# First attention: two units taken together, both scored, a pair multiplied by the values, another pair turned

## The chip, the cores and the metric

The kernel runs on one core of a Trainium2 chip. The metric is the device time of one execution in microseconds (us). Five engines matter: PE (TensorE: matmuls and transposes), PEld (its weight loads, shown as a row of their own), DVE (VectorE), ACT (ScalarE), POOL (GpSimd), and the DMA queues, of which SP's carries most loads.

## The reference

A model of three blocks with 1024 channels, on 1024 latent tokens and 256 context tokens. The change lies in the first block's attention, which has two parts, both computed for every tile of 128 query tokens:

- part A: 8 heads of 64 with 2 key heads (four heads share one). A latent query sees the keys of its own block of 128, of the blocks on either side where they are within 128 tokens, and all 256 context keys; a context query sees the context keys alone. A sink value joins the sum of each softmax.
- part B: 4 heads with two score sets each, `w = softmax(s1) - lam * softmax(s2)`, and `w @ v` with values of 128. A latent query sees all 1280 keys, a context query the 256 context keys.

Cut to what matters:

```python
def sink_attention(qg, k, v, sink, valid):
    s = einsum('bqhgd,bkhd->bhgqk', qg, k) * 64 ** -0.5
    s = where(valid, s, NEG_INF)
    p = softmax(concatenate([s, sink_col], -1), -1)[..., :-1]
    return einsum('bhgqk,bkhd->bqhgd', p, v)

def diff_attention(q1, q2, k1, k2, v, lam):
    s1 = einsum('bqhd,bkhd->bhqk', q1, k1) * 64 ** -0.5
    s2 = einsum('bqhd,bkhd->bhqk', q2, k2) * 64 ** -0.5
    w = softmax(s1, -1) - lam * softmax(s2, -1)
    return einsum('bhqk,bkhe->bqhe', w, v)
```

The outputs of both parts are normed and gated, and go through an output matrix in the next stage.

## The kernel before

`layer0` first projects queries, keys, values and gates and stores them in device memory, then does the attention. There are ten query tiles, in the order `ORD` = 0, 1, 2, 3, 8, 9, 4, 5, 6, 7; 8 and 9 are the context tiles. Each tile has two halves of six units: four A heads (`a_scores`) and two B heads (`b_scores`), in the order A0, B0, A1, A2, B1, A3 (the very first half begins with B0, A0). That makes 120 units. A unit has three steps:

- scores, at once when `a_scores` or `b_scores` is called. PE multiplies queries by keys (L685, L687 for A, L730, L731 for B) in single-pass fp32r; for a latent A unit one or two bf16 matmuls add the window masks (L690, L692). DVE reads the scores out of PSUM with their minimum (L695; L732, L734), ACT takes the exponentials (L697; L736, twice for B), and for B DVE combines both score sets (L740, L741, L742). The weights stand then in a tile `Pa` or `Pb0`.
- `turns`: PE transposes the weights, block by block of 128 keys (L663, in `turn`; five blocks for a latent A unit of an inner tile, four in tiles 0 and 7, two for context queries; ten for B, two for context queries). ACT copies the result out of PSUM into `PTa` or `PTb` (L665), for B's second group DVE does (L667).
- `outs`: PE multiplies the transposed weights by the values. A does it in two halves of 64 columns that stand side by side in the array (L710, a 128x64 form); B with whole columns of 128 (L754).

```python
                for j, b in enumerate(kbl):
                    for u in range(2):
                        nc.tensor.matmul(t.o[64 * u:64 * u + 64, hh * 64:(hh + 1) * 64], PT[:, j, 64 * u:64 * u + 64],
                                         V[:, b, g * 64:(g + 1) * 64], start=(j == 0), stop=(j == len(kbl) - 1))
```

An fp32 matmul by values runs as two instructions, so a latent A unit has 20 of L710 (16 in tiles 0 and 7, 8 for context queries) and a latent B unit 20 of L754.

PSUM has eight banks: two buffers `sc` of two banks for the large scores (an A unit takes one, a B unit one for each of its score sets e0 and e1), one buffer `scc` for the 256 context scores of B, and three buffers `tp` for transposed blocks, one of which holds the half's output `t.o` from the first `outs` to `half_end`. In SBUF there are four `Pa`, two of each `Pb`, three `PTa` and two `PTb`. `half_end` scales, norms and gates a half's output on DVE, ACT and POOL. `head_of_tile` loads the next tile's queries `Q` (L582, four transfers on SP's queue) and gates.

The loop at the end of `layer0` is a hand-written pipeline over units. In step n it scores unit n, turns unit n - 3 (`LAGA` = 3) and multiplies unit n - 4 by the values; `half_end` follows each sixth unit, and the head of the next tile is loaded in step 8 of the 12 of a tile. After the last scores the query buffers are given back, and `Bridge` begins with the output stage: it loads its weights, and one step later transposes the first attention output (L876).

The order on each engine is that in which the compiler's scheduler places the instructions: mostly the written order, but where an instruction isn't ready by its account (a buffer that isn't free yet), later ones go ahead.

Of the kernel before, what the change touches and what calls it, by code (L numbers as in the profile page):

```python
# [23 lines left out]
EPS = 1e-6  # L24
NEG = -1e30
LAM0 = 0.2
LAGA = 3
ORD = (0, 1, 2, 3, 8, 9, 4, 5, 6, 7)
WB = 8

# [262 lines left out]
def rstd_of(k, pool, ss, n, inv_n, name):  # L293

    nc = k.nc
    r = pool.tile([128, n], F32, name=name)
    nc.vector.tensor_scalar(r, ss, inv_n, EPS, op0=OP.mult, op1=OP.add)
    nc.gpsimd.tensor_tensor(r, r, k.mhalf[:, :n], op=OP.pow)
    return r
# [146 lines left out]
def layer0(k, x, ctxt):  # L446
# [13 lines left out]
    with ExitStack() as es:  # L460
# [116 lines left out]
        def load_q(i):  # L577

            Q = qp.tile([128, 16, 2, 128], F32R, name="Q", bufs=2)
            for part in range(2):  # L580
                for u in (0, 64):
                    nc.sync.dma_start(Q.bitcast(F32)[u:u + 64, :, part, :], dq[i][64 * part:64 * part + 64])  # L582
            return Q
# [51 lines left out]
    with ExitStack() as es:  # L635
# [12 lines left out]
        def head_of_tile(i):  # L648

            t = Ctx()  # L650
            tiles[i] = t
            t.Q = Q0 if i == order[0] else load_q(i)
            t.gt = p.tile([128, 1024], F32, name="gt", bufs=2)
            nc.sync.dma_start(t.gt, dg[i])
            t.mt = p.tile([128, 1024], F32, name="mt", bufs=2)
            t.sta = p.tile([128, 8, 4], F32, name="sta", bufs=2)
            t.stb = p.tile([128, 4, 8], F32, name="stb", bufs=2)
            t.o = None
# [99 lines left out]
        def half_end(i, hg):  # L758

            t = tiles[i]  # L760
            ca, cb = slice(256 * hg, 256 * hg + 256), slice(512 + 256 * hg, 768 + 256 * hg)
            h4, h2 = slice(4 * hg, 4 * hg + 4), slice(2 * hg, 2 * hg + 2)
            es_ = p.tile([128, 4], F32, name="esk", bufs=2)
            nc.vector.tensor_add(es_, sink[:, h4], t.sta[:, h4, 0])
            nc.scalar.activation(es_, es_, AF.Exp)
            nc.vector.tensor_add(es_, es_, t.sta[:, h4, 2])
            rl = p.tile([128, 6], F32, name="rl", bufs=2)
            nc.vector.reciprocal(rl[:, 0:4], es_)
            nc.vector.reciprocal(rl[:, 4:6], t.stb[:, h2, 2])
            ma, mb = t.mt[:, ca], t.mt[:, cb].rearrange("p (h d) -> p h d", d=128)  # L770
            nc.vector.tensor_mul(ma.rearrange("p (h d) -> p h d", d=64), t.o[:, 0:256].rearrange("p (h d) -> p h d", d=64),  # L771
                                 rl[:, 0:4, None].to_broadcast([128, 4, 64]))
            nc.vector.tensor_mul(mb, t.o[:, 256:512].rearrange("p (h d) -> p h d", d=128), rl[:, 4:6, None].to_broadcast([128, 2, 128]))
            t.o = None
            nc.gpsimd.tensor_mul(ma, ma, t.gt[:, ca])  # L775
            sq = p.tile([128, 2, 128], F32, name="sqb", bufs=1)
            ss = p.tile([128, 2], F32, name="ssb", bufs=2)
            nc.gpsimd.tensor_mul(sq, mb, mb)
            nc.vector.tensor_reduce(ss, sq, axis=AX.X, op=OP.add)
            rr = rstd_of(k, p, ss, 2, 1.0 / 128, "rrb")  # L780
            nc.gpsimd.tensor_mul(mb, mb, subg[:, None, :].to_broadcast([128, 2, 128]))
            nc.gpsimd.tensor_mul(t.mt[:, cb], t.mt[:, cb], t.gt[:, cb])
            nc.vector.tensor_mul(mb, mb, rr[:, :, None].to_broadcast([128, 2, 128]))
            if hg:
                nc.sync.dma_start(dm[i], t.mt)

        units = []
        order = list(ORD)
        for i in order:
            for hg in range(2):  # L790
                a, b = 4 * hg, 2 * hg
                u = [(a_scores, i, a), (b_scores, i, b), (a_scores, i, a + 1), (a_scores, i, a + 2), (b_scores, i, b + 1),
                     (a_scores, i, a + 3)]
                if not units:
                    u[0], u[1] = u[1], u[0]
                units += u
        head_of_tile(order[0])
        fs = []
        for n in range(len(units) + LAGA + 1):
            if n < len(units):  # L800
                f, i, h = units[n]
                fs.append(f(i, h))
                if n % 12 == 8 and i != order[-1]:
                    head_of_tile(order[n // 12 + 1])
            if n == len(units):

                es0.close()
                k.slots = Slots(k)
                br = Bridge(k, 0, (0, 1), dm, NTC)
                br.fetch(p.tile([128, S + L], F32, name="Pb1", bufs=2)[:, :D])  # L810
                br.start(k.slots)
            if 0 <= n - LAGA < len(units):
                fs[n - LAGA][0]()
            j = n - LAGA - 1
            if j >= 0:
                fs[j][1]()
                if j % 6 == 5:
                    half_end(units[j][1], j // 6 % 2)
            if n == len(units) + 1:
                br.first(lambda: ps.tile([128, 4, 128], F32, name="tp", bufs=3),  # L820
                         lambda b: p.tile([128, 2, 4, 128], F32R, name=("gt", "mt")[b], bufs=2))
    br.es = es2
# [1452 lines left out]
def body(tc, nc, A, out):  # L2275
    k = Ctx()
    k.tc, k.nc, k.A, k.ndma = tc, nc, A, 0
    squeeze(A)
    tiles = lambda ap, n: [ap[i * 128:(i + 1) * 128, :] for i in range(n)]
    with ExitStack() as es:  # L2280
        setup(k, es)
        x1, x2 = ([k.dr.tile([128, D], F32, name=f"{n}_{i}") for i in range(NT)] for n in ("x1", "x2"))
        x, ctxt = tiles(A["x"], NT), tiles(A["ctx"], 2)
        br = layer0(k, x, ctxt)
        br = layer1(k, br, x, ctxt, x1)
        dm = mixer2(k, br, x1, x2)
        moe(k, dm, x2, tiles(out, NT))
# [27 lines left out]
```

## Time and profile before

| | |
|---|---|
| median of 3 runs | 2800.44 us (2799.43 to 2801.71) |
| profiled execution, its own time | 2795.24 us |
| its span | 2793.5 us |
| mean granted TensorE clock | 0.979 of 2.4 GHz |
| PE busy | 2645.3 us (95% of the span) |
| DVE, ACT, POOL busy | 1536.0, 1066.6, 580.9 us |

The attention runs from about 487 to 858 us of the span. In the rows of PE a matmul's duration contains its way through the array, and the next one starts before it ends; what a group of matmuls takes is read from its start to the start of the next group.

### The profile page before, as it was taken

Reading aid. Unit: us, or ns where it says so; the run is one execution under the profiler, and the core shown is the slowest. Engines: PE = TensorE matmul, PEld = TensorE weight load, DVE = VectorE, ACT = ScalarE, POOL = GpSimd, SP = SyncE. Lnnn points to the kernel's source line nnn. Section 1 sums busy time; section 2 is a strip of 40 time slices with the busy share of each in tenths; the row PEclk is TensorE's granted clock in tenths of the full one; section 3 lists DMA queues with packets and bytes.
Section 4 is the critical chain, followed back from the end, with each engine's and each line's share of the span. In section 5 each row is a group of like instructions: output and inputs, shape, how many; then the busy total and the mean of one; then the engine's idle time right before and its main releaser. Section 6 shows DMA issues by size and latency. Waiting matters only on the chain. (4 is left out here: it accounts for less than half of the span.)

```text
span 2793.5 us, 41767 instructions
## 1 busy us (share of the span) xinstructions
PE 2645.3 (95%) x15970; PEld 2172.5 (78%) x15970; DVE 1536.0 (55%) x2972; ACT 1066.6 (38%) x2035; POOL 580.9 (21%) x515
## 2 busy tenths in 40 slices
PE   8999999999999999999999999999999999969995
PEld 3777778887887778887887887788878977857774
DVE  5467747887886461100884434373206655357886
ACT  4333321666663332112642332222316621246563
POOL 1334400012211110012541120000000033025662
PEclk9999999999999999999999999999999999979998
DMA  7233387546224353222654123232437157449995
GB/s 249 83 90 106 114 214 213 183 92 121 66 51 164 108 184 106 86 76 101 200 193 151 60 84 106 91 117 83 125 122 174 32 165 253 143 171 325 312 317 173
DMA packets 273570, 405.33 MB, mean 145 GB/s; under 512 B 28338, under 2 KB 156585, under 8 KB 272721
## 3 DMA queue, kind: packets, MB, share of 16 engines
q1 hardware_dynamic: 255360, 365.79, 42.7%
q0 software_dynamic: 6624, 24.14, 3.4%
q10 hardware_dynamic: 11376, 12.64, 1.4%
q8 instruction: 128, 2.10, 0.3%
q14 instruction: 82, 0.66, 0.1%
HBM read 290.35 MB, written 112.15 MB: 144 GB/s over the span
## 5 line engine op out<-in xcount | busy, mean ns | idle before, releaser
L164 DVE TENSOR_TENSOR slotl<-slotraw,sloth 128x1024 fp32r<-128x1024 f32 (+2 forms) x100 | 116.8, 1170 | 282.7 <-ACT sloth L161 226.6
L168 PE MATMUL pj<-sloth,u2h 128*128 128x512 f32 (+1 forms) x592 | 237.4, 401 | 0.0
L169 PE MATMUL pj<-slotl,u2h 128*128 128x512 f32 (+1 forms) x592 | 234.8, 397 | 0.0
L170 PE MATMUL pj<-sloth,u2l 128*128 128x512 f32 (+1 forms) x592 | 233.2, 394 | 0.0
L168 PE MATMUL pj<-wh,h0h 128*128 128x512 f32 (+1 forms) x560 | 216.2, 386 | 0.3 <-DVE h0h L338 0.3
L169 PE MATMUL pj<-wl,h0h 128*128 128x512 f32 (+1 forms) x560 | 212.3, 379 | 0.5 <-DVE wl L164 0.4
L170 PE MATMUL pj<-wh,h0l 128*128 128x512 f32 (+1 forms) x560 | 211.4, 378 | 0.0
L169 PE MATMUL pj<-slotl,h1h 128*128 128x512 f32 x432 | 168.7, 391 | 0.0
L168 PE MATMUL pj<-sloth,h1h 128*128 128x512 f32 x432 | 168.7, 390 | 0.0
L170 PE MATMUL pj<-sloth,h1l 128*128 128x512 f32 x432 | 168.5, 390 | 0.0
L161 ACT CAST sloth<-slotraw 128x1024 fp32r<-128x1024 f32 (+2 forms) x100 | 99.6, 999 | 152.8 <-PE my L170 62.5
L168 PEld LDWEIGHTS pj<-sloth,u2h 128*128 128x128 f32 (+1 forms) x592 | 110.0, 186 | 28.3 <-issue 1.0
L170 PEld LDWEIGHTS pj<-sloth,u2l 128*128 128x128 f32 (+1 forms) x592 | 110.0, 186 | 28.3
L169 PEld LDWEIGHTS pj<-slotl,u2h 128*128 128x128 f32 (+1 forms) x592 | 110.0, 186 | 26.8 <-issue 1.0
L168 PEld LDWEIGHTS pj<-wh,h0h 128*128 128x128 f32 x560 | 106.7, 191 | 20.7 <-issue 2.0
L169 PEld LDWEIGHTS pj<-wl,h0h 128*128 128x128 f32 x560 | 107.1, 191 | 19.4 <-DVE wl L164 1.6
L170 PEld LDWEIGHTS pj<-wh,h0l 128*128 128x128 f32 x560 | 106.4, 190 | 19.6
L164 DVE TENSOR_TENSOR w13l<-raw,w13h 128x1024 fp32r<-128x1024 f32 x51 | 106.0, 2092 | 1.6 <-ACT w13h L161 1.1
L736 ACT ACTIVATE Pb<-Pb,stb 128x1280 f32<-128x1280 f32 (+1 forms) x80 | 94.9, 1188 | 29.9 <-DVE stb L735 29.6
L168 PE MATMUL pj<-sloth,omTh 128*128 128x512 f32 x256 | 103.3, 404 | 0.5 <-ACT omTh L161 0.5
L775 POOL TENSOR_TENSOR mt<-mt,gt 128x256 f32<-128x256 f32 x20 | 14.7, 737 | 422.9 <-DVE mt L771 219.6
L170 PE MATMUL pj<-sloth,omTl 128*128 128x512 f32 x256 | 101.6, 398 | 0.0
(614 smaller groups left out, 6707.9 us busy)
## 6 DMA issues: line engine op xcount, KB each, us to landing
raw<-in_exp_w_dram SPq DMA_DIRECT2D x102, 512.0 KB
Q<-dq SPq DMA_DIRECT2D x40, 512.0 KB
slotraw<-in_w_in_dram SPq DMA_DIRECT2D x40, 512.0 KB
mraw<-in_adaln_w_dram SPq DMA_DIRECT2D x64, 256.0 KB
wraw<-in_ab_w_in_dram SPq DMA_DIRECT2D x24, 512.0 KB
slotraw<-in_gla_w_in_dram SPq DMA_DIRECT2D x24, 512.0 KB
fg<-po SPq DMA_DIRECT2D x48, 256.0 KB
g<-fg SPq DMA_DIRECT2D x16, 768.0 KB
```

What stands on the lines that cost most here:

```text
L161: nc.scalar.copy(hi, src)
L164: (nc.vector if lo_eng == "v" else nc.gpsimd).tensor_sub(lo, src, hi.bitcast(F32))
L168: nc.tensor.matmul(out, lh, rh, start=first, stop=False)
L169: nc.tensor.matmul(out, lh, rl, start=False, stop=False)
L170: nc.tensor.matmul(out, ll, rh, start=False, stop=last)
L736: nc.scalar.activation(P[:, :nk], P[:, :nk], AF.Exp, bias=mc, scale=-1.0, accum_out=sm)
L775: nc.gpsimd.tensor_mul(ma, ma, t.gt[:, ca])
```

## The change

`LAGA` goes, and the pipeline is written over 60 pairs of units. A half's pairs are (A0, B0), (A1, A2) and (B1, A3). In step n both units of pair n are scored, then pair n - 2 is multiplied by the values, B units ahead of A units (`sorted` by "is it an A unit", which keeps the order of equals), then pair n - 1 is turned. `half_end` follows the products of each third pair, the next tile's head is loaded in step 4 of the 6 of a tile (after the scores of the units counted 8 and 9 from zero; before, after unit 8). The transposes of the output stage's first tile are written at the end of the step after the last scores. No instruction is added or left out, and no buffer changes.

```diff
-LAGA = 3
...
+        pairs = [units[n:n + 2] for n in range(0, len(units), 2)]
         fs = []
-        for n in range(len(units) + LAGA + 1):
-            if n < len(units):
-                f, i, h = units[n]
-                fs.append(f(i, h))
-                if n % 12 == 8 and i != order[-1]:
-                    head_of_tile(order[n // 12 + 1])
-            if n == len(units):
+        for n in range(len(pairs) + 2):
+            if n < len(pairs):
+                fs.append([(f is a_scores, f(i, h)) for f, i, h in pairs[n]])
+                i = pairs[n][0][1]
+                if n % 6 == 4 and i != order[-1]:
+                    head_of_tile(order[n // 6 + 1])
+            if n == len(pairs):
 
                 es0.close()
                 k.slots = Slots(k)
                 br = Bridge(k, 0, (0, 1), dm, NTC)
                 br.fetch(p.tile([128, S + L], F32, name="Pb1", bufs=2)[:, :D])
                 br.start(k.slots)
-            if 0 <= n - LAGA < len(units):
-                fs[n - LAGA][0]()
-            j = n - LAGA - 1
+            j = n - 2
             if j >= 0:
-                fs[j][1]()
-                if j % 6 == 5:
-                    half_end(units[j][1], j // 6 % 2)
-            if n == len(units) + 1:
+                for _, f in sorted(fs[j], key=lambda u: u[0]):
+                    f[1]()
+                if j % 3 == 2:
+                    half_end(pairs[j][0][1], j // 3 % 2)
+            if 0 <= n - 1 < len(pairs):
+                for _, f in fs[n - 1]:
+                    f[0]()
+            if n == len(pairs):
                 br.first(...)
```

## Rows read from the trace of the kernel before

**Rows 1.** Busy time of each engine in two stretches, granted clock, DMA.

```profile
core 0: us, PE busy (x) PEld busy (x) DVE busy (x) ACT busy (x) POOL busy (x), PEclk, DMA share, GB/s
...
520.00:648.60 128.60, 128.60 (x1297) 112.94 (x1295) 110.32 (x315) 85.76 (x179) 24.30 (x35) 1.00 0.41 85
...
673.00:677.00 4.00, 3.58 (x22) 3.22 (x23) 2.49 (x16) 2.71 (x9) 0.00 (x0) 0.57 1.23 189
```

**Rows 2.** Timeline of PE within one half of an inner latent tile.

```profile
start us, us, engine line op out<-in xcount [idle before <-releaser]
599.54 0.73 PE L730 MATMUL sc<-K,Q 128*128 128x512 f32 x2
...
601.74 1.25 PE L663 MATMUL tp<-ident,Pb 128*128 128x128 f32 x10
602.85 0.50 PE L731 MATMUL scc<-K,Q 128*128 128x256 f32 x2
603.28 0.80 PE L710 MATMUL tp<-V,PTa 128*64 128x64 f32 x20
604.02 0.44 PE L685 MATMUL sc<-K,Q 128*128 128x384 f32 x1
604.30 0.28 PE L687 MATMUL sc<-K,Q 128*128 128x256 f32 x1
604.41 0.34 PE L685 MATMUL sc<-K,Q 128*128 128x384 f32 x1
604.59 0.28 PE L687 MATMUL sc<-K,Q 128*128 128x256 f32 x1
...
604.78 0.22 PE L692 MATMUL sc<-mkb,idb 128*128 128x128 bf16 x1
604.83 0.60 PE L663 MATMUL tp<-ident,Pa 128*128 128x128 f32 x4
...
611.06 1.10 PE L730 MATMUL sc<-K,Q 128*128 128x512 f32 x4
612.00 0.93 PE L663 MATMUL tp<-ident,Pb 128*128 128x128 f32 x7
```

**Rows 3.** Timeline of PE in the first tile: three A units' products together.

```profile
501.35 1.62 PE L710 MATMUL tp<-V,PTa 128*64 128x64 f32 x48
502.90 0.74 PE L730 MATMUL sc<-K,Q 128*128 128x512 f32 x2
```

**Rows 4.** Timeline of PE in tile 7: transposes ahead of either kind of product.

```profile
836.62 0.60 PE L663 MATMUL tp<-ident,Pa 128*128 128x128 f32 x4
837.05 1.73 PE L754 MATMUL tp<-V,PTb 128*128 128x128 f32 x14
838.54 0.36 PE L685 MATMUL sc<-K,Q 128*128 128x256 f32 x1
...
839.16 0.61 PE L663 MATMUL tp<-ident,Pa 128*128 128x128 f32 x4
839.70 0.69 PE L710 MATMUL tp<-V,PTa 128*64 128x64 f32 x16
```

**Rows 5.** Timeline of PE at the stage's end: transposes between products by halves.

```profile
851.33 0.45 PE L710 MATMUL tp<-V,PTa 128*64 128x64 f32 x6
851.70 0.44 PE L663 MATMUL tp<-ident,Pb 128*128 128x128 f32 x2
852.07 0.56 PE L710 MATMUL tp<-V,PTa 128*64 128x64 f32 x10
```

**Rows 6.** Timeline of PE: scores straight after a mask.

```profile
608.28 0.22 PE L692 MATMUL sc<-mkb,idb 128*128 128x128 bf16 x1
608.31 0.72 PE L730 MATMUL sc<-K,Q 128*128 128x512 f32 x2
608.86 0.74 PE L663 MATMUL tp<-ident,Pa 128*128 128x128 f32 x5
```

**Rows 7.** Timeline of DVE: the combination of the B unit of rows 2.

```profile
608.04 1.55 DVE L742 SCALAR_TENSOR_TENSOR Pb<-Pb,stb,Pb 128x1280 f32<-128x1280 f32 x1
```

**Rows 8.** What SP's queue waited for in the stage: total us, times, longest.

```profile
SPq L582 <- PE sc L692: 102.6, 5, 20.5
```

**Rows 9.** What PE waited for in the stage, 487 to 862 us.

```profile
PE tp L663 <- DVE Pb L742: 6.2, 4, 3.0
```

## The prediction

> **What bounds the kernel now.** I read the table of stretches first. The change touches one stage, the first attention, which runs from about 487 to 858 us. In its middle, 520 to 648.6 us, PE is busy for 128.60 of 128.60 us at granted clock 1.00, that is at 2.4 GHz, while DVE is busy 86% and ACT 67% of it [rows 1]. So PE sets the pace there, and what a tuner can win is PE time: columns, or what PE loses between kinds of work. But a busy PE is not PE at its peak, so I then read PE's timeline by start times: the distance from one group's start to the next is what the group really costs.
>
> One half of a latent tile is six units: four of kind A (scores against K0, five transposes, products by halves, 20 matmuls of 64 columns) and two of kind B (scores in two parts e0 and e1, ten transposes, 20 whole products). Call the kinds of PE work R (scores), M (masks), T (transposes), O (whole products, L754) and H (products by halves, L710). In the written order each A unit has its H alone, between the T of a later unit and the R of a still later one [rows 2]. That shows where PE loses time although it counts as busy:
>
> - Inside an H run. 20 in one run take 603.28 to 604.02 = 0.74 us [rows 2]; 48 in one run, three units of the first tile that happen to stand together, take 501.35 to 502.90 = 1.55 us [rows 3]. So a further matmul costs 0.81 / 28 = 29 ns and a run has 0.74 - 20 x 0.029 = 0.16 us of its own.
> - Entering H. Four T ahead of H take 839.16 to 839.70 = 0.54 us, four ahead of O 0.43 us [rows 4]: 0.11 us.
> - Leaving H. The first score after it takes 604.02 to 604.30 = 0.28 us, the same shape two later 0.18 us [rows 2]: 0.10 us. If T follows instead, two T between two H runs take 851.70 to 852.07 = 0.37 us [rows 5]; less 0.11 for entering and 2 x 0.109 for the T themselves, 0.04 to 0.05 us is left.
>
> An H run thus costs 0.37 us beside its products if scores follow and 0.32 us if transposes follow. Leaving O is nothing: 14 O and the handover take 837.05 to 838.54 = 1.49 us, 0.106 each [rows 4].
>
> **The change, part by part.** It alters no arithmetic and no number of instructions, only the order.
>
> *Fewer H runs.* The pairs of a half are (A0, B0), (A1, A2), (B1, A3). A1's and A2's products now stand together, so four runs become three. There are 20 halves (10 tiles), 80 A units; the first half has three units in one run already [rows 3], so 78 runs become 60. 18 fewer at 0.32 to 0.37 us, I take 0.34: -6.2 us.
>
> *What follows an H run.* Products are now followed by the pair turned, so the way out of H is into T and not into R: 60 runs x 0.05 us = -3.0 us as written; 0 if scores get in between. I take -3.0, since the written order is what PE has to do next.
>
> At this place the Trainium skill has a rule: the page "TensorEngine Tiling (Array Packing)", section "Key Properties", says that changing the tiling mode drains the TensorE. The rows agree that a change costs, but by that rule alone every change would cost the same whatever stands after it: the first term would stay at -6.2 us, the second would be 0, and the sum below 3.0 us smaller.
>
> *Masks.* A's scores end in bf16 masks. Before, T mostly followed, at no cost. Scores straight after a mask cost more: two score matmuls take 608.31 to 608.86 = 0.55 us against 2 x 0.235 (611.06 to 612.00, four) = 0.47, while the mask hands over after 0.03 us (608.28) instead of 0.05 (604.78 to 604.83, to T) [rows 2, 6]: about +0.05 us. In the new order it occurs after A0, A1, A2 and A3 (scores or products follow), before once per half [rows 6]: three more in 16 latent halves, 48 x 0.05 = +2.4 us. The trace has mask-to-score; mask-to-product I take as equal; the lower bound is 0.
>
> *Waits for slots.* Score tiles have two buffers, the small one one. e1's small score waits until DVE has read e0's: e1's large scores end at 601.74, and the small ones come at 602.85 [rows 2]; ten T fill the 1.1 us. Afterwards something else must fill it (first rival); where it does I take 0. Two transposed units in a row ask more of the buffers that T writes; next in order are then the scores of the next pair, and rows show T and R changing places in mid-unit (T x10, R x2) [rows 2], so I take 0 with that cover; without it, it would be a stall of some tenths per pair.
>
> *Query loads.* The next tile's queries are issued after the scores of unit 10 instead of 9 of the tile. SP's entry waits for PE's scores of the tile before to free the buffer, not for its place in the program [rows 8], so 0. The output stage's weights still start after the last scores: 0. Beginning and end of the stage I take as unchanged.
>
> **Sum:** -6.2 - 3.0 + 2.4 = -6.8 us; with the terms at their bounds, from -5.8 + 0 + 2.4 = -3.4 to -6.7 - 3.0 + 0 = -9.7 us. After the stage PE goes on with projections that wait for its end, so the gain is carried. The profiled execution took 2795.24 us (span 2793.5), the median of the runs is 2800.44, 0.2% more; a difference of this size carries over as it is: 2800.44 - 6.8 = 2793.6 us.
>
> **Rivals.**
>
> *The merged run is cut again.* With (A0, B0) scored together, e1's small scores wait as before, about 0.8 to 1.1 us, and the next thing in order is now the H run of (A1, A2), 0.16 + 40 x 0.029 = 1.3 us long. PE's order is not the written one where something isn't ready: the small scores stand behind ten T that were written after them [rows 2], and an H run of 16 is cut into 6 and 10 by T [rows 5]. If the small scores are put into the run, four H runs per half stay and the first term is gone: -0.6 us, 2799.8. Against it: if DVE is still busy with A0's scores, it may read the small tile first, and the wait is gone. Chance 0.27.
>
> *B's chain comes late (slower).* B0's first score starts at 599.54; its combined weights are done at 608.04 + 1.55 = 609.59 [rows 2, 7]: 10.05 us, through DVE, ACT and DVE again. T starts at 612.00, so 2.4 us were to spare. In the new order PE has between that start and T(B0): B0's scores 2.4 (599.54 to 601.74 and the two small ones), H of A1 and A2 1.3 + 0.15, T of B1 and A3 15 x 0.109 = 1.6, scores of A1 and A2 2 x 0.81 = 1.6 (604.02 to 604.83), O of B1 20 x 0.106 = 2.1, H of A3 0.74 + 0.15, T of A0 0.55: 10.6 us. Some 0.55 us are to spare. A0's scores now stand directly ahead of B0's in DVE's queue, and DVE also has the reads of A1 and A2 to do before the combination. If the chain becomes longer than 10.6 us, PE stalls by the excess in each of 16 latent halves: at 11.0 us the gain is gone (0.4 x 16 = 6.4), from 11.4 us on the kernel is over 0.2% slower; at 11.4 us it is 0.8 x 16 - 6.8 = +6.0 us, 2806.4. For it: PE waited for this very combination four times, 6.2 us, in the stage [rows 9]. Against: none of them falls in 520 to 648.6 us, where PE has no idle time [rows 1], and scores of the next pair can fill in. Chance 0.17.
>
> *The order hardly changes.* What PE runs differs from the written order already [rows 2, 5]; if the placement by readiness gives nearly the same stream, the time stays within 3 us of before: 2799. Chance 0.07.
>
> *The clock falls.* In 673 to 677 us, among the short context tiles, the granted clock is 0.57, so PE is at 1.2 GHz for most of it [rows 1]; Were one such stretch to come in each of the 20 halves, 4.0 x 0.43 = 1.7 us each, it would be +34 us less 6.8: 2828. Nothing in the latent tiles (1.00 throughout, T runs of ten included) speaks for it. Chance 0.02.
>
> **How the numbers follow.** Forecast 0.47, rivals 0.27, 0.17, 0.07, 0.02. A measurement of this kernel tells about 0.2%, 5.6 us, from no change. The forecast case gives faster, but for the part near its bound of -3.4; some of the others win the waits for slots too: faster 0.45, same 0.37, slower 0.18. The likeliest case alone spans 2790.7 to 2797.0. The range takes in the cut run, most of the late chain's smaller sizes, and on the low side the waits that may vanish (0.2 us in 16 halves, 3 us beyond -9.7): 2787 to 2804.
>
> **What would show it.** Right: H runs of 40 and 60 runs in all; T after H; a half of a latent tile 0.3 to 0.4 us shorter; PE's busy stretch still whole. Wrong: small scores between two H runs of 20 (cut run); PE idle before T of Pb, released by the combination L742 (late chain); H runs as before (no change); a granted clock under 1.00 in the latent tiles.

## The result and the profile after

The changed kernel took 2838.94 us (median of 4 runs, 2831.24 to 2843.64), the kernel before 2801.07 us beside it (4 runs, 2799.43 to 2801.72): ratio 1.0141, interval 1.0127 to 1.0154. It is slower, by some 38 us, and outside the range given. The profiled execution took 2841.1 us (span 2839.3).

I measure the stage from its first score to the first projection that follows it. Two rows of the table of stretches, one of each kernel, split the loss; columns as in [rows 1]. The kernel before:

```profile
484.85:858.35 373.50, 358.71 (x3512) 311.11 (x3513) 307.49 (x932) 245.36 (x549) 67.42 (x96) 0.98 0.45 105
```

The changed kernel, the stage and two stretches within it:

```profile
491.32:901.95 410.63, 370.90 (x3513) 325.73 (x3513) 310.08 (x932) 246.99 (x548) 68.34 (x96) 0.95 0.41 97
...
574.00:594.00 20.00, 17.95 (x189) 15.77 (x188) 14.91 (x41) 12.47 (x29) 3.42 (x5) 1.00 0.76 138
594.00:597.40 3.40, 3.40 (x19) 3.31 (x18) 2.73 (x11) 2.25 (x3) 0.00 (x0) 0.52 0.27 111
```

The stage is 37.1 us longer. PE idles 39.7 us of it instead of 14.8, 24.9 us more; and it is busy 12.2 us longer with the same matmuls. The two short stretches show both: in 574 to 594 us PE, never idle at this place before [rows 1], idles 2.05 us, and then the granted clock is 0.52 for 3.4 us. Such a stretch at 1.2 GHz occurs 12 times in the stage, four times before. Each costs about 3.4 x 0.48 = 1.6 us: eight more are 13.1 us, less some 8 x 0.34 = 2.7 us for 72 H runs instead of 80 (both counted in the traces): 10.4 of the 12.2 us. The other 1.8 us are of the size of the handovers between kinds of work, which the part on the prediction comes to.

PE's timeline of one half shows the place of the idle time (compare [rows 2]):

```profile
start us, us, engine line op out<-in xcount [idle before <-releaser]
577.97 1.09 PE L729 MATMUL sc<-K,Q 128*128 128x512 f32 x4
578.99 0.45 PE L709 MATMUL tp<-V,PTa 128*64 128x64 f32 x8
579.37 0.50 PE L730 MATMUL scc<-K,Q 128*128 128x256 f32 x2
579.81 1.15 PE L709 MATMUL tp<-V,PTa 128*64 128x64 f32 x32
...
587.15 0.76 PE L662 MATMUL tp<-ident,Pa 128*128 128x128 f32 x5
587.67 0.71 PE L729 MATMUL sc<-K,Q 128*128 128x512 f32 x2
588.22 1.25 PE L662 MATMUL tp<-ident,Pb 128*128 128x128 f32 x10
...
589.44 0.63 PE L729 MATMUL sc<-K,Q 128*128 128x512 f32 x2
...
590.02 1.10 PE L729 MATMUL sc<-K,Q 128*128 128x512 f32 x4
590.96 0.60 PE L753 MATMUL tp<-V,PTb 128*128 128x128 f32 x4
593.61 0.44 PE L684 MATMUL sc<-K,Q 128*128 128x384 f32 x1 [2.05 <-DVE Pb L733]
...
602.02 1.09 PE L729 MATMUL sc<-K,Q 128*128 128x512 f32 x4
```

Two things are to be seen. The merged H run is cut, 8 and 32, by e1's small scores (L730). And B1's scores e0 and e1 (up to 590.96) fill both score buffers; A3's scores (L684), now due right behind them, need e0's, and wait 2.05 us until DVE has read it (L733). Only four whole products stand between. From this half's start to the next it is 602.02 - 577.97 = 24.05 us; before, 599.54 [rows 2] to the same scores at 620.07 were 20.53. The same wait stands in the half ahead of this one and in the half behind it:

```profile
571.17 0.44 PE L684 MATMUL sc<-K,Q 128*128 128x384 f32 x1 [2.06 <-DVE Pb L733]
...
617.67 0.44 PE L684 MATMUL sc<-K,Q 128*128 128x384 f32 x1 [2.06 <-DVE Pb L733]
```

From 571.17 to the same place at 593.61 are 22.44 us, with the clock at 1.00 up to 594 us; from there to 617.67, with the half-clock stretch in it, 24.06. So the wait and the clock can be told apart: the clock's share is 1.62 us.

Why DVE reads e0 late, its timeline tells (line numbers are one lower than before):

```profile
587.27 0.42 DVE L770 TENSOR_TENSOR mt<-tp,rl 128x256 f32<-128x256 f32 x1 [0.33 <-PE tp L709]
...
589.11 0.42 DVE L778 TENSOR_REDUCE ssb<-sqb 128x2 f32<-128x256 f32 x1 [1.08 <-POOL sqb L777]
...
591.39 0.42 DVE L782 TENSOR_TENSOR mt<-mt,rrb 128x256 f32<-128x256 f32 x1 [1.48 <-POOL rrb L297]
591.73 0.68 DVE L666 COPY PTb<-tp 128x512 f32<-128x512 f32 x1
592.33 1.22 DVE L733 TENSOR_SCALAR_CACHE_REDUCE Pb<-sc 128x1024 f32<-128x1024 f32 x1
```

and POOL's timeline, the two products (L780, L781) and the power (L297) of the same norm:

```profile
589.15 0.73 POOL L780 TENSOR_TENSOR mt<-mt,subg 128x256 f32<-128x256 f32 x1
589.97 0.73 POOL L781 TENSOR_TENSOR mt<-mt,gt 128x256 f32<-128x256 f32 x1
590.66 0.70 POOL L297 TENSOR_TENSOR rrb<-rrb,mhalf 128x2 f32<-128x2 f32 x1
```

DVE's rows up to L782 belong to `half_end`. DVE goes through its queue in order: it waits 1.08 us for POOL's squares and 1.48 us for POOL's power, which POOL runs behind two products, and starts nothing else meanwhile. e0 is finished at 590.07 (589.44 + 0.63), but its read stands in DVE's queue behind all this and a copy: it comes at 592.33, 5.06 us after L770.

In the kernel before, `half_end` comes directly before the next B unit's scores, and DVE had the read (L734 there) ahead of the norm's reduction (L779 there), as DVE's timeline of before shows:

```profile
599.66 0.42 DVE L771 TENSOR_TENSOR mt<-tp,rl 128x256 f32<-128x256 f32 x1 [0.27 <-PE tp L710]
...
600.89 1.22 DVE L734 TENSOR_SCALAR_CACHE_REDUCE Pb<-sc 128x1024 f32<-128x1024 f32 x1 [0.48 <-PE sc L730]
...
602.04 0.41 DVE L779 TENSOR_REDUCE ssb<-sqb 128x2 f32<-128x256 f32 x1
```

Over the whole stage the table of waits of the changed kernel has (total us, times, longest):

```profile
PE sc L684 <- DVE Pb L733: 24.4, 17, 2.1
PE tp L662 <- DVE Pb L741: 7.0, 5, 3.0
```

and that of the kernel before, for the first of these waits:

```profile
PE sc L685 <- DVE Pb L734: 2.2, 6, 0.8
```

The first wait is 22.2 of the 24.9 us that PE idles more. The second row is the wait for B's combination, much as before [rows 9].

### The profile page after: what moved, and what is told of

It reads as the page before. It is cut to its first block, busy times and chain, and to the rows that moved or that the text cites. A ratio compares the mean times of both kernels' runs of the same rounds, so it can differ in the third digit from the quotient of the medians.

```text
span 2839.3 us, 41778 instructions
## 1 busy us (share of the span) xinstructions
PE 2664.2 (94%) x15970; PEld 2193.3 (77%) x15970; DVE 1538.7 (54%) x2972; ACT 1067.8 (38%) x2035; POOL 582.6 (21%) x515
## 5 line engine op out<-in xcount | busy, mean ns | idle before, releaser
L168 PE MATMUL pj<-slotl,omTh 128*128 128x512 f32 x256 | 102.1, 399 | 0.0
```

Source lines behind the costliest of these rows:

```text
L168: nc.tensor.matmul(out, lh, rl, start=False, stop=False)
```

## The experiments

All ratios are against the kernel before, with their 95% interval.

**1. The norm behind the next scores.** The changed kernel; `half_end`'s second part is held back until DVE's last large-score read of the next pair is issued. PE's order stays nearly that of the changed kernel.

```diff
+                    read[:] = [nc.vector.tensor_scalar(P[:, :S], sx, ...)]
...
+            def rest():
                 nc.vector.tensor_reduce(ss, sq, axis=AX.X, op=OP.add)
                 ...
+            return rest
...
-                    half_end(pairs[j][0][1], j // 3 % 2)
+                    norm.append(half_end(pairs[j][0][1], j // 3 % 2))
...
+            if norm:
+                with tc.issue_after(read[0].ins):
+                    norm.pop()()
```

> The changed kernel, but the half's second part (the reduction of the squares, the power, the two products on POOL, the last product and the store) is written one step later and its DVE instructions are held behind DVE's reads of the next B unit's large scores. Theory 'norm ahead' (DVE waits some 2.6 us a half for POOL's part of the norm, and the read that frees a score buffer stands behind it in DVE's queue): PE's wait before A3's scores, 2.05 us in a half now, goes, the half-clock stretches in the latent tiles go with it, and the time comes back to 2793 to 2803. Theory 'two scored units want a third score buffer' (A3 right behind B1 has to wait for the read of e0 whatever DVE does before): over 1 us a half stays, 2820 or more. Theory 'longer chain to the transposes': no change, 2835 to 2842.

Measured: 2794.63 us (10 runs) against 2795.75, 0.9993 [0.9982, 1.0004]. The stage takes 371.5 us, 39.1 less than in the changed kernel. DVE's timeline of this kernel (its L780 and L784 are the reduction and the last product):

```profile
581.11 0.42 DVE L770 TENSOR_TENSOR mt<-tp,rl 128x256 f32<-128x256 f32 x1 [0.53 <-PE tp L709]
...
583.95 1.23 DVE L733 TENSOR_SCALAR_CACHE_REDUCE Pb<-sc 128x1024 f32<-128x1024 f32 x1
...
587.82 0.41 DVE L780 TENSOR_REDUCE ssb<-sqb 128x2 f32<-128x256 f32 x1
...
589.31 0.43 DVE L784 TENSOR_TENSOR mt<-mt,rrb 128x256 f32<-128x256 f32 x1 [0.74 <-POOL rrb L297]
```

the whole stage and a stretch of inner latent tiles:

```profile
486.93:858.46 371.53, 354.68 (x3513) 311.93 (x3513) 304.13 (x932) 245.95 (x549) 68.07 (x96) 0.99 0.45 106
520.00:643.00 123.00, 122.94 (x1257) 109.57 (x1255) 104.59 (x301) 83.93 (x178) 21.24 (x31) 1.00 0.42 87
```

and PE's scores of A3:

```profile
584.81 0.60 PE L753 MATMUL tp<-V,PTb 128*128 128x128 f32 x4
585.24 0.44 PE L684 MATMUL sc<-K,Q 128*128 128x384 f32 x1
```

e0 is read 2.84 us after L770 and not 5.06, PE is idle for 0.06 of 123 us in the inner latent tiles, and there the clock stays at 2.4 GHz. A3's scores still come behind B1's and four whole products, as in the changed kernel, and don't wait: a third scored unit alone, with two buffers, does not make the wait. DVE still waits for POOL (0.74 us), but nothing that PE needs stands behind it. A half takes 20.36 us (B scores at 581.51 to the same at 601.87), and 20.36 + 2.05 + 1.6 gives 24.0, the 24.05 of the changed kernel. There are 71 H runs. So the norm's place in DVE's order makes the whole loss; and with the norm elsewhere the new order gains nothing that can be told from no change.

**2. Turn first.** The pair is turned ahead of the products, so `half_end` stands next to the following scores, as in the kernel before.

```diff
+            if 0 <= n - 1 < len(pairs):
+                for _, f in fs[n - 1]:
+                    f[0]()
             j = n - 2
...
-            if 0 <= n - 1 < len(pairs):
-                for _, f in fs[n - 1]:
-                    f[0]()
```

> The changed kernel with the pair turned before the earlier pair is multiplied, so that the half's end stands directly ahead of the next pair's scores as it did before the change. Theory 'norm ahead': DVE reads e0 of B1 before it comes to the norm (their order in DVE's queue says so), the wait before A3's scores is under 0.5 us a half, 2793 to 2805. Theory 'third score buffer': A3 still follows B1, 2820 or more.

Measured: 2809.11 us (8 runs), 1.0049 [1.0034, 1.0064]: a miss. The waiting went as expected (3.2 us in the stage instead of 24.4, no further half-clock stretches), but the transposes, now ahead, cut the H runs. PE's timeline:

```profile
572.24 0.45 PE L709 MATMUL tp<-V,PTa 128*64 128x64 f32 x6
572.61 0.44 PE L662 MATMUL tp<-ident,Pb 128*128 128x128 f32 x2
572.98 0.69 PE L709 MATMUL tp<-V,PTa 128*64 128x64 f32 x16
```

The stage has 114 H runs, 34 more than before: 34 x 0.34 = 11.6 of the 14.0 us by which it is longer (387.5 us).

**3. The kernel before, its read held behind the norm.** To make the wait where it was not.

```diff
+                    with ExitStack() as hold:
+                        if held and not e:
+                            hold.enter_context(tc.issue_after(held.pop().ins))
-                    nc.vector.tensor_scalar(P[:, :S], sx, ...)
+                        nc.vector.tensor_scalar(P[:, :S], sx, ...)
...
-            nc.vector.tensor_mul(mb, mb, rr...)
+            held[:] = [nc.vector.tensor_mul(mb, mb, rr...)]
```

> The kernel before, unit by unit, with one thing from the changed one: DVE's read of the large scores e0 of the first B unit after a half's end is held behind the last product of that half's norm. Theory 'norm ahead': this alone makes PE wait 1.5 to 3 us in each of 16 latent halves, with a half-clock stretch after some: 2825 to 2860. Theory 'third score buffer': without two units scored together there is no such wait, 2800 to 2808.

Measured: 2812.52 us (4 runs), 1.0047 [1.0031, 1.0064], a miss. PE doesn't wait as in the changed kernel: its waits for these reads are 2.8 us, the longest 0.8. DVE's timeline of one half, and PE's scores of A3 in it:

```profile
588.34 1.21 DVE L737 TENSOR_SCALAR_CACHE_REDUCE Pb<-sc 128x1024 f32<-128x1024 f32 x1
...
589.90 0.42 DVE L786 TENSOR_TENSOR mt<-mt,rrb 128x256 f32<-128x256 f32 x1 [0.34 <-POOL rrb L298]
...
590.20 0.44 PE L685 MATMUL sc<-K,Q 128*128 128x384 f32 x1
590.24 1.22 DVE L737 TENSOR_SCALAR_CACHE_REDUCE Pb<-sc 128x1024 f32<-128x1024 f32 x1
```

One large read stands ahead of the norm's last product (L786) and one behind it; by the hold the late one is e0's. A3's scores start before that read does, so the early read had freed a buffer for them. The compiler had also placed the work on PE otherwise: 107 H runs, 27 more, 27 x 0.34 = 9.2 of the 14.7 us by which the stage grew (388.2). So the experiment did not make the wait; it neither shows the wait's price nor speaks against it.

**4. A3 ahead of B1** in the third pair.

```diff
-                u = [..., (b_scores, i, b + 1), (a_scores, i, a + 3)]
+                u = [..., (a_scores, i, a + 3), (b_scores, i, b + 1)]
```

> The changed kernel with the third pair as (A3, B1), A3 scored first. Theory 'third score buffer': A3 has a buffer at once and e1 gets A3's, whose read is short, as in the first pair, which doesn't stall: 2797 to 2810. Theory 'norm ahead': the reads still stand behind the norm, and now e1's scores wait for A3's: 2825 to 2850.

Measured: 2817.78 us (4 runs), 1.0069 [1.0052, 1.0086], between what the theories asked. The norm still stands ahead of the reads (in 520 to 650 us DVE waits four times for the power, 4.9 us). But PE's waits are shorter and spread: it is busy 125.59 of the 130 us from 520 to 650, and the granted clock is 1.00 there. H runs: 73. The stage takes 389.1 us.

**5. The same with the norm behind** (experiment 1 with A3 ahead of B1).

> The first experiment (norm behind the reads) with the third pair as (A3, B1). With the norm ahead of the reads this order gave 1.0069. Theory 'norm ahead': with the norm out of the way the order of the pair matters little, ratio 0.997 to 1.002, as many runs of products by halves as in the first experiment (71). Rival 'the third pair as (A3, B1) is slow by itself': 1.005 or more.

Measured: 2796.09 us (12 runs) against 2798.02, 1.0001 [0.9987, 1.0015]. With the norm out of the way the order of the third pair doesn't matter, and the loss of experiment 4 is gone too. That pair decided only what the late read struck.

**6. A smaller dose.** The changed kernel; the norm's two products on POOL are written after DVE's last product, so POOL runs the power straight after the squares.

```diff
+            nc.vector.tensor_mul(mb, mb, rr[:, :, None].to_broadcast([128, 2, 128]))
             nc.gpsimd.tensor_mul(mb, mb, subg...)
             nc.gpsimd.tensor_mul(t.mt[:, cb], t.mt[:, cb], t.gt[:, cb])
-            nc.vector.tensor_mul(mb, mb, rr[:, :, None].to_broadcast([128, 2, 128]))
```

> The changed kernel with the norm's two products on POOL written behind DVE's last product instead of ahead of it (the same factors in another order), so that DVE waits for the squares and the power alone, no longer for all of POOL's part. The power-first run did not shorten the wait, since DVE's last product reads what the two products write; this one does. DVE's order stays: the norm ahead of the read of e0. Theory 'DVE waits for POOL ahead of the read': the read of e0 starts some 4.2 us after the half's end instead of 5.1, the wait before A3's scores falls from 2.05 to about 1.2 us, some half-clock stretches go: 2808 to 2830, ratio 1.004 to 1.011. Rival 'only the place in the queue counts': ratio 1.0125 or more.

Measured: 2811.82 us (5 runs), 1.0045 [1.0029, 1.0061]. PE's order is that of the changed kernel, with the same 72 H runs. DVE's timeline:

```profile
579.90 0.42 DVE L770 TENSOR_TENSOR mt<-tp,rl 128x256 f32<-128x256 f32 x1 [0.33 <-PE tp L709]
...
581.74 0.42 DVE L778 TENSOR_REDUCE ssb<-sqb 128x2 f32<-128x256 f32 x1 [1.08 <-POOL sqb L777]
...
583.17 0.42 DVE L780 TENSOR_TENSOR mt<-mt,rrb 128x256 f32<-128x256 f32 x1 [0.81 <-POOL rrb L297]
...
584.11 1.21 DVE L733 TENSOR_SCALAR_CACHE_REDUCE Pb<-sc 128x1024 f32<-128x1024 f32 x1
...
601.50 0.42 DVE L770 TENSOR_TENSOR mt<-tp,rl 128x256 f32<-128x256 f32 x1 [0.34 <-PE tp L709]
```

The stretch of inner latent tiles:

```profile
520.00:646.00 126.00, 121.10 (x1231) 107.36 (x1229) 103.44 (x295) 82.06 (x173) 21.55 (x32) 1.00 0.42 85
```

and PE's wait for the read in its table of waits, 520 to 650 us:

```profile
PE sc L684 <- DVE Pb L733: 4.8, 4, 1.2
```

The read comes 4.21 us after L770, 0.85 sooner than in the changed kernel, and PE's wait is 1.2 us, 0.84 shorter. The clock stays at 1.00, and a half takes 21.60 us: 20.36 + 1.2. So the length of the wait follows the length of the norm's chain on DVE. The fall of the clock followed nine of the ten idle times of 2.05 us in the changed kernel, and none of the ten of 1.2 us here.

**7. POOL's products held behind the power**, the same aim by another way.

```diff
+            power = nc.gpsimd.tensor_tensor(rr, rr, k.mhalf[:, :2], op=OP.pow)
+            with tc.issue_after(power.ins):
                 nc.gpsimd.tensor_mul(mb, mb, subg...)
                 nc.gpsimd.tensor_mul(t.mt[:, cb], t.mt[:, cb], t.gt[:, cb])
```

> The changed kernel with one order turned round on POOL alone: the power of the norm, for which DVE waits, ahead of the two products on POOL instead of behind them. DVE's queue still has the norm ahead of the read of e0. Theory 'DVE waits for POOL ahead of the read': the read of e0 comes some 1.2 us sooner, the wait before A3's scores falls from 2.05 to about 0.8 us a half and part of the half-clock stretches go: 2805 to 2825, ratio 1.002 to 1.009. Rival 'only the place of the norm in DVE's queue counts, not how long it waits': within 0.2% of the changed kernel, ratio 1.012 or more.

Measured: 2841.26 us (4 runs), 1.0167 [1.0137, 1.0198], a miss, and the fault is the experiment's. DVE's last product multiplies what POOL's products leave, so it waited for them in place of the power. DVE's timeline:

```profile
585.49 0.42 DVE L770 TENSOR_TENSOR mt<-tp,rl 128x256 f32<-128x256 f32 x1 [0.33 <-PE tp L709]
...
590.27 0.43 DVE L785 TENSOR_TENSOR mt<-mt,rrb 128x256 f32<-128x256 f32 x1 [1.72 <-POOL mt L784]
590.61 0.42 DVE L731 TENSOR_SCALAR_CACHE_REDUCE Pb<-scc 128x256 f32<-128x256 f32 x1
590.95 1.22 DVE L733 TENSOR_SCALAR_CACHE_REDUCE Pb<-sc 128x1024 f32<-128x1024 f32 x1
```

The read comes 5.46 us after L770, later than in the changed kernel, PE waits up to 2.2 us (14 times, 21.8 us in the stage, for the small tile's read L731 in the same queue), and there are 12 half-clock stretches again, four of them 6.8 us long. The chain not shortened, the loss stayed.

**8. The merged run kept whole.** Experiment 1, and the products of A1 and A2 held on PE behind the small score that cut them.

```diff
+                        if j % 3 == 1:
+                            hold.enter_context(tc.issue_after(small[0].ins))
                         f[1]()
```

> The kernel of the first experiment (norm behind the reads), and the products by halves of A1 and A2 held on PE behind e1's small scores of the B unit scored just before, so that nothing cuts their run: 60 runs of products by halves instead of 71. Theory 'each run costs 0.34 us': 11 x 0.34 = 3.7 us less than the first experiment, 0.15 to 0.25% less than the kernel before, ratio 0.9975 to 0.9990. Rival 'runs are free, the cut one filled a wait': PE now waits for the small scores with nothing to do, ratio 0.9990 to 1.0015.

Measured: 2799.77 us (12 runs), 1.0013 [0.9999, 1.0027], a miss. There are 60 H runs, as the prediction wanted. But a new row stands in the table of waits:

```profile
PE tp L662 <- ACT PTa L664: 4.5, 9, 0.5
```

The transposes of B's weights now wait for a buffer that ACT has not yet copied. Against experiment 1, 11 runs fewer are worth 11 x 0.34 = 3.7 us. PE is indeed busy 2.6 us less in the stage than there, but idle 4.2 us more. So the piece of the H run that went ahead had been filling a wait.

**9. The two products apart.** Experiment 1 with one unit's transposes put between A1's and A2's products.

```diff
+                    if m and j % 3 == 1 and n - 1 < len(pairs):
+                        fs[n - 1][0][1][0]()
                     f[1]()
```

> The kernel of the first experiment with the products of A1 and A2 parted by a unit's transposes, as single units would be: 99 runs of products by halves instead of 71. Theory 'each run costs 0.34 us': 28 x 0.34 = 9.5 us more than the first experiment, ratio 1.0020 to 1.0045 to the kernel before. Rival 'runs are free': as the first experiment, ratio 0.998 to 1.0010.

Measured: 2804.99 us (12 runs), 1.0034 [1.0021, 1.0047]. 99 H runs, 28 more than in experiment 1; the stage is 379.2 - 371.5 = 7.7 us longer, 0.28 us for each, and by the ratios (0.0041 x 2796 = 11.5 us) 0.41. So an H run has a price, near the 0.34 us of the prediction.

## Why the prediction was wrong

*"Waits for slots", taken as 0: the step that failed.* The text saw that a score buffer is read late (1.1 us filled by ten transposes [rows 2]) and asked only what PE would put into that time. It did not ask when DVE would get to the read. Two moves of the change belong there and were not priced. B1 is followed at once by A3, so the third score tile in a row needs e0's buffer; and `half_end` is now followed by the transposes of a pair and only then by B1's scores, so its norm, with two waits for POOL, enters DVE's queue ahead of e0's read. In the stage this cost 24.4 us of waiting, 2.2 before. Experiment 1 takes it away and with it the loss; experiment 6 shortens it by 0.85 us a half and PE's wait by 0.84; experiment 7 doesn't shorten it, and the loss stays. These show the cause. Experiment 3, which was to make the wait in the kernel before, made none.

*"The clock falls", chance 0.02.* The text saw in [rows 1] what the clock does among the short context tiles, priced a stretch at 1.7 us (about 1.6 was measured) and gave 2828 for one in every half. But it took full PE stretches in the latent tiles as given, where a wait of the step above could take them away. Wait and clock go together: 24.9 us of idle time and eight more half-clock stretches, 13.1 us, less 2.7 us of H runs, make 35.3 of the 37.1 us.

*"Fewer H runs", -6.2 us: mis-sized.* The price of a run held (experiments 2 and 9); the number did not. The kernel before had 80 runs in its trace, not 78, the changed one has 72 and not 60, since e1's small scores cut the merged run into 8 and 32: the rival "the merged run is cut again" came true inside the slower outcome. Worth 8 x 0.34 = 2.7 us. Keeping the run whole (experiment 8) gave nothing, since PE then waited instead.

*"What follows an H run" and "Masks": right in kind, but a term is missing beside them.* In experiment 1, where the rest can be seen without the wait, 52 runs end in transposes (7 before: 45 x 0.05 = -2.3 us), and masks are followed by scores or products 58 times (20 before: 38 x 0.05 = +1.9 us). With 9 H runs fewer (-3.1 us) that makes -3.5 us. But what follows the transposes was left out. Scores follow transposes 100 times in experiment 1 and 39 times before, and there two large scores of B take 0.55 us (587.67 to 588.22 in PE's timeline of the changed kernel), as after a mask, against the 0.47 of the prediction. By estimate, at the same 0.05 us, 61 more are +3.1 us (+2.2 with the 17 fewer that follow whole products at the same price): most of what the other three terms give. So the way into scores was not saved, it was moved. The stage of experiment 1 is 2.0 us shorter than before all the same, but two stretches at 1.2 GHz touch it, 7.6 us in all, where the kernel before had four, 13.7 us: at half speed that is about 3 us; and PE idles 2.1 us more. Even with no wait, then, the new order itself was worth next to nothing, and not 6.8 us; the ratio of 0.9993, between 0.9982 and 1.0004, fits that.

*"B's chain comes late", chance 0.17.* It didn't: 7.0 us of waits on the combination against 6.2 [rows 9], and in most halves none. (The unit whose chain the text read from 599.54 on is B1, not B0: the ten transposes at 601.74 are B0's. The length of the chain is a B unit's in either case.)

Open stays a part of the profiled difference: the span is 45.8 us longer and the stage 37.1. The stage begins 6.5 us later, at 491.3 us, behind code that is the same; in the nine experiments' profiles, again with the same code ahead, it began anywhere between 482.2 and 488.1 us. Why it began so late here, no run shows.

## What to carry to other kernels

When an epilogue is moved, list for each engine what its instructions now stand ahead of: DVE's instruction that waits for POOL holds up every read behind it, and the read that frees PE's buffer may be one of them. A buffer wait is priced by when the reader gets to it, through its queue, and not by how soon the data are ready; an epilogue that nobody waits for goes behind the reads. A run that the placement cuts may be filling a wait, so that joining it brings the wait back. And where a new order avoids one handover between kinds of work, count the handovers that it puts in its place.

## What was unexpected in the hardware's rows

An idle time of PE of about 2 us in a half mostly brought 3.4 us at 1.2 GHz with it (granted clock 0.50 to 0.52): nine times of ten in the changed kernel, eight of ten in experiment 7 (1.98 to 2.2 us). One of 1.2 us (experiment 6) did not, in ten of ten. Where the clock fell, a wait of 2.05 us cost some 3.7 (2.05 + 1.6). The length of the idle time alone does not decide: among the context tiles the clock fell after 1.57 us in the kernel before (at 700 us), and not after 1.67 us in experiment 2 (at 705 us).

POOL's small instructions are long beside DVE's: the power of 128 x 2 elements takes 0.70 us, about as long as a product of 128 x 256 (0.73); DVE has 0.42 us for a product of that size. A chain that goes from DVE to POOL and back twice, as this norm does, takes over 4 us from L770 to its last product (587.27 to 591.39), 2.56 us of which DVE stood idle.
